# Two buffers in place of one for the query tile in the second part of the differential attention

## The chip, the cores and the metric

The kernel runs on one core of a Trainium2 chip. The metric is the device time of one launch in microseconds (us). Most executions of a kernel agree within 0.3%. Engine names in the views are PE (TensorE, matmuls), PEld (its weight loads), DVE (VectorE), ACT (ScalarE), POOL (GpSimd) and SP (SyncE). All transfers between memory and the on-chip buffer in this kernel are issued by SP, which serves its queue in order.

## The reference

One layer of a hybrid streaming encoder is computed for a prompt of 2048 tokens and a sample of 32 tokens, all in float32. Group A of the attention is a differential attention with four heads: each head has two query and key maps of 64 dimensions and one value of 128.

```python
def diff_core(q, k, v, bias, mask, lam):
    s = jnp.einsum('bqhmd,bkhmd->bhmqk', q, k).astype(jnp.float32) * (HEAD_DIM ** -0.5) + bias[:, None]
    s = jnp.where(mask, s, NEG)
    p = jax.nn.softmax(s, axis=-1)
    w = p[:, :, 0] - lam * p[:, :, 1]
    return jnp.einsum('bhqk,bkhe->bqhe', w.astype(v.dtype), v)

def merge(oa, ob, subln_g, out_norm_b, w_out, lam_init):
    ...
    return jnp.concatenate([oa.reshape(B, T, WIDTH_A), ob], axis=-1) @ w_out

def ffn_ple(h, p, g_mlp, w_up, w_down, w_ple_gate, w_ple_proj):
    c = rmsnorm(h, g_mlp)
    h = h + jnp.square(jax.nn.relu(c @ w_up)) @ w_down
    return h + jax.nn.sigmoid(h @ w_ple_gate) * (p @ w_ple_proj)
```

The mask is causal by chunks of 64 tokens, so a later query sees more keys. Group B is a band attention with eight heads over the last eight chunks. Both groups are projected from the normed input by `w_in`, merged by `w_out`, and followed by the MLP and a gated embedding. The queries, keys and values also leave the kernel as outputs.

## The kernel before

**Numbers.** Every matrix product is made in float32 precision from split operands: a value is stored as a rounded high part and a low part, and a product takes three matmuls (`mm3`, lines L168 to L170). In the attention, high and low parts lie in the two halves of the 128 partitions, or in two planes of a tile.

**Order of the stages.** Tokens are worked on in four blocks of 512 (the last with the sample's 32 behind it). The program projects the queries, keys and values of the first half, does the first part of the differential attention (query pairs 0 to 3) with `self.small = True`, then the rest of the projections and the band attention. After that it sets `self.small = False` and opens the pool `a1` for the second part:

```python
JA1 = [(4, 5), (6, 7, 8)]
            with ExitStack() as x:
                pool = opened(x, "a1", 1, side="right")
                for js in JA1:
                    self.attn_a(js, pool, ps_s, ps_t, ps_o)
```

A pair `j` is two query tiles of 128 tokens; pair 8 stands for the sample. For each group of pairs and each of four heads, `attn_a` loads the bias (`ba`) and the keys (`ka`, one buffer: four transfers for pairs 4 and 5, six for pairs 6 to 8), and then handles the pairs one after another: 20 query tiles in all, eight of them at the start of a head. Each pair loads its queries (`q`, by `load_q`, four transfers), makes score matmuls (tile `s`, L545, three accumulators `ps_s`), row maxima, exponentials in `e` (two buffers for the first map, one for the second), the combination of both maps, transposes (`tpp`, L617), and the products with the values (`v`, two buffers, loaded in chunks; L631 to L633). The result is stored to `oT`.

**What runs beside it.** What follows in the program is the output projection of blocks 0 and 1, their MLP (`ups` and `dps`) and the gate of block 1 (`gps`, `pps`), on two accumulators (`mm`). The program's instructions are put in order by a planner when it is built: it plays the program on a model of the chip, and where an engine would be free it takes an instruction that is ready, the earliest in the program first. So the MLP fills the engines while the second part of the attention waits. In the finished program the order on each engine and on SP's queue is fixed. A buffer that is taken again is guarded by a wait.

**Memory.** The query tile has 2 maps x 2 parts x 256 queries of 4 bytes, so 4 KB in each partition. In the program before, the pool `a1` occupies the upper end of each partition's memory from byte 149,728 to 229,344, and the highest pool from the other side that is in use beside it (`uq`, the MLP's) ends at byte 143,904. Between them 5,824 bytes are free.

The band attention calls `load_q` too, but only while `self.small` is true.

Of the kernel before, what the change touches and what calls it, by code (L numbers as in the profile page):

```python
# [13 lines left out]
F32R = mybir.dt.float32r  # L14
# [5 lines left out]
P = 128  # L20
# [112 lines left out]
class Kern:  # L133
# [343 lines left out]

    def load_q(self, pool, gi, t0, n, maps):
        nc = self.nc
        q = pool.tile([P, len(maps), 2, 256], F32R, tag="q", bufs=2 if self.small else 1, name="q")  # L480
        for d in range(2):
            for i, m in enumerate(maps):
                self.dma(
                    q[64 * d : 64 * d + 64, i, :, :n],
                    self.qS[gi, :, 64 * m : 64 * m + 64, t0 : t0 + n].rearrange("l r c -> r l c"),
                )
        return q
# [796 lines left out]
```

## Time and profile before

| | |
|---|---|
| time, median of 3 runs | 3329.38 us (3328.49 to 3332.86) |
| the profiled execution's own time | 3334.02 us |
| its span, first to last instruction | 3332.1 us |
| mean granted TensorE clock | 0.969 |
| PE busy | 3111.6 us (93%) |
| DVE, ACT, POOL busy | 1674.4, 1705.5, 1467.9 us |
| moved by DMA | 488.93 MB, mean 147 GB/s |
| score matmuls of the second part (L545) | from 1367.3 to 2173.8 us |

A row of a group of instructions reads: line, engine, operation, output and inputs by the program's names, shape and count, then busy time and the mean duration in ns, then the idle time of the engine just before them and what ended it. In a timeline, "[2.16 <-DMA q<-qS]" means that the engine was idle for 2.16 us until the load of `q` had landed. A row of the waits gives the total, the number of times and the longest. A row of the windows gives the stretch and its length, the busy time of PE, PEld, DVE, ACT and POOL with the number of instructions in brackets, and then the clock that TensorE was granted, the busy share of the DMA engines and GB/s. A row of the transfers gives the size of one and the median time from its issue to its landing in us. "issue" is time in which an engine waited for nothing that the profile shows, and SPq is SP's queue.

### The profile page before, as it was taken

The page shows a single profiled execution, that of the slowest core. Times are in us where ns is not written, and L with a number is a line of the kernel's source. Part 1 is how long each engine was busy: PE and PEld are TensorE (multiplying, and loading weights), DVE is VectorE, ACT ScalarE, POOL GpSimd, SP SyncE. Part 2 cuts the span into 40 slices and gives each one's busy share as a digit, 9 for nine tenths or more (in the row PEclk, how much of TensorE's full clock was granted, in tenths as well). Part 3 has the DMA queues.
Part 4 walks back from the last instruction along what each step waited for, and adds up shares of the span by engine and source line. Part 5 has one row for each costly group of instructions (what it writes and reads, how often), then busy time and mean ns, then how long its engine had stood idle before and what let it go on. Part 6 is the DMA issues. An engine that isn't in the chain of part 4 may idle for free.

```text
span 3332.1 us, 50114 instructions
## 1 busy us (share of the span) xinstructions
PE 3111.6 (93%) x17881; PEld 2723.4 (82%) x17881; DVE 1674.4 (50%) x3952; ACT 1705.5 (51%) x3717; POOL 1467.9 (44%) x1083
## 2 busy tenths in 40 slices
PE   6988989999999999989899999988989999999998
PEld 6877778889877888778787878877779999999987
DVE  5117777454555544566656665746542322223235
ACT  4226666566665666666666665654443223222245
POOL 4335654432324433534544443555753333333365
PEclk9998899999999999999999999999999999999999
DMA  7488777786788554544644454346631111111133
GB/s 227 160 253 235 214 212 202 213 241 205 209 238 234 159 139 126 143 137 133 197 134 123 129 136 130 121 135 222 181 114 51 45 45 45 45 47 49 45 91 102
DMA packets 519074, 488.93 MB, mean 147 GB/s; under 512 B 37885, under 2 KB 414017, under 8 KB 518825
## 3 DMA queue, kind: packets, MB, share of 16 engines
q1 hardware_dynamic: 518824, 485.73, 50.2%
q8 instruction: 142, 2.33, 0.3%
q14 instruction: 108, 0.88, 0.1%
HBM read 379.06 MB, written 110.49 MB: 147 GB/s over the span
## 4 chain that ended last, share of the span: by engine, by line
PE 71%; DMA 12%; DVE 7%; ACT 3%; issue 3%; POOL 2%; SPq 2%; DVEq 0%; POOLq 0%; ACTq 0%
PE dps L168 6%; PE dps L169 6%; PE dps L170 6%; PE ups L168 6%; PE ups L169 6%; PE ups L170 6%; PE s L545 3%; DMA q<-qS 3%; PE qps L168 3%; PE qps L169 3%; PE qps L170 3%; PE ob L744 2%; PE sb L704 2%; SPq L144 2%; DMA ka<-kS 2%
## 5 line engine op out<-in xcount | busy, mean ns | idle before, releaser
L153 POOL TENSOR_TENSOR wl<-wr,wh 128x1024 fp32r<-128x1024 f32 x338 | 819.8, 2427 | 1027.5 <-ACT wh L149 985.3
L949 DVE TENSOR_TENSOR h<-h,dps 128x512 f32<-128x512 f32 (+1 forms) x640 | 373.1, 585 | 590.9 <-PE dps L170 578.4
L149 ACT ACTIVATE wh<-wr 128x1024 fp32r<-128x1024 f32 x338 | 357.4, 1058 | 539.9 <-PE dps L169 294.8
L168 PE MATMUL dps<-uh,wh 128*128 128x512 f32 (+1 forms) x1280 | 460.6, 360 | 14.8 <-DVE h L949 11.1
L168 PE MATMUL ups<-cH,wh 128*128 128x512 f32 (+1 forms) x1280 | 452.5, 354 | 9.3 <-ACT relu L914 7.7
L170 PE MATMUL dps<-uh,wl 128*128 128x512 f32 (+1 forms) x1280 | 453.0, 355 | 0.0
L169 PE MATMUL dps<-ul,wh 128*128 128x512 f32 (+1 forms) x1280 | 453.0, 354 | 0.0
L170 PE MATMUL ups<-cH,wl 128*128 128x512 f32 (+1 forms) x1280 | 451.9, 353 | 0.0
L169 PE MATMUL ups<-cL,wh 128*128 128x512 f32 (+1 forms) x1280 | 451.9, 353 | 0.0
L168 PEld LDWEIGHTS dps<-uh,wh 128*128 128x128 f32 x1280 | 243.8, 190 | 49.8 <-DVE h L949 16.9
L168 PEld LDWEIGHTS ups<-cH,wh 128*128 128x128 f32 x1280 | 242.2, 189 | 41.3 <-ACT relu L914 7.9
L170 PEld LDWEIGHTS dps<-uh,wl 128*128 128x128 f32 x1280 | 242.9, 190 | 33.4
L169 PEld LDWEIGHTS ups<-cL,wh 128*128 128x128 f32 x1280 | 242.7, 190 | 31.1
L153 POOL TENSOR_TENSOR ul<-relu,uh 128x272 fp32r<-128x272 f32 (+1 forms) x160 | 176.0, 1100 | 206.3 <-ACT uh L149 203.6
L170 PEld LDWEIGHTS ups<-cH,wl 128*128 128x128 f32 x1280 | 242.3, 189 | 30.1
L169 PEld LDWEIGHTS dps<-ul,wh 128*128 128x128 f32 x1280 | 243.2, 190 | 27.0
L545 PE MATMUL s<-ka,q 128*128 128x256 f32 (+4 forms) x784 | 197.2, 357 | 50.4 <-DMA q<-qS 29.1
L168 PE MATMUL qps<-aH,wh 128*128 128x512 f32 (+1 forms) x640 | 230.2, 360 | 6.6 <-ACT wh L149 2.2
L169 PE MATMUL qps<-aL,wh 128*128 128x512 f32 (+1 forms) x640 | 228.3, 357 | 0.0
L170 PE MATMUL qps<-aH,wl 128*128 128x512 f32 (+1 forms) x640 | 227.9, 356 | 0.0
L559 ACT ACTIVATE e<-s,nm 128x512 f32<-128x512 f32 (+3 forms) x256 | 155.2, 611 | 102.7 <-DVE nm L551 65.2
L545 PEld LDWEIGHTS s<-ka,q 128*128 128x128 f32 (+1 forms) x784 | 137.4, 200 | 78.5 <-issue 27.3
(217 smaller groups left out, 7076.9 us busy)
## 6 DMA issues: line engine op xcount, KB each, us to landing
wr<-w_up SPq DMA_DIRECT2D x96, 512.0 KB, 4.2
wr<-w_down SPq DMA_DIRECT2D x96, 512.0 KB, 3.7
wr<-w_in SPq DMA_DIRECT2D x74, 512.0 KB, 4.9
q<-qS SPq DMA_DIRECT2D x256, 128.0 KB, 4.7
v<-vSa SPq DMA_DIRECT2D x64, 512.0 KB, 3.8
ka<-kS SPq DMA_DIRECT2D x32, 512.0 KB, 7.2
wr<-w_out SPq DMA_DIRECT2D x32, 512.0 KB, 5.0
wr<-w_ple_gate SPq DMA_DIRECT2D x32, 512.0 KB, 4.4
```

The lines of the kernel that those rows point to most:

```text
L144: self.nc.sync.dma_start(dst, src)
L149: nc.scalar.activation(hi, raw, AF.Copy)
L153: eng.tensor_tensor(lo, raw, hi.bitcast(F32), op=ALU.subtract)
L168: nc.tensor.matmul(ps, lh, rh, start=start and i == 0, stop=False)
L169: nc.tensor.matmul(ps, lh, rl, start=False, stop=False)
L170: nc.tensor.matmul(ps, ll, rh, start=False, stop=stop and i == n - 1)
L545: nc.tensor.matmul(s, q[:, m, hl, P * qi : P * qi + nr], kt[:, m, k0 : k0 + n], start=hl == 0, stop=hl == 1)
L559: nc.scalar.activation(dst, src, AF.Exp, bias=nmx, accum_out=z[:nr, m, bi : bi + 1])
L704: nc.tensor.matmul(s, q[:, 0, hl, P * qi : P * qi + nr], kt[:, c : c + w], start=hl == 0, stop=hl == 1)
L744: nc.tensor.matmul(o[:, qa:qb], vt, pt[:kn, i - kfirst, qa:qb], start=x == 0 and y == 0, stop=x == len(order) - 1 and y == 1,)
L949: nc.vector.tensor_tensor(hv, hv, ps, op=ALU.add)
```

## The change

`load_q` asks for two buffers of the query tile whatever `self.small` is. Only the second part of the differential attention had one; in the first part and in the band attention there were two before. The pool `a1` grows by 4,096 bytes in each partition.

```diff
     def load_q(self, pool, gi, t0, n, maps):
         nc = self.nc
-        q = pool.tile([P, len(maps), 2, 256], F32R, tag="q", bufs=2 if self.small else 1, name="q")
+        q = pool.tile([P, len(maps), 2, 256], F32R, tag="q", bufs=2, name="q")
         for d in range(2):
             for i, m in enumerate(maps):
```

## The prediction, made before the changed kernel was built

> **What bounds the kernel now.** I read the page first, for the engine that carries the span; then the waits of that engine in the stretch that the change touches; then single instructions at the places found.
>
> ```profile
> span 3332.1 us, 50114 instructions
> PE 3111.6 (93%) x17881; PEld 2723.4 (82%) x17881; DVE 1674.4 (50%) x3952; ACT 1705.5 (51%) x3717; POOL 1467.9 (44%) x1083
> PEclk9998899999999999999999999999999999999999
> L545 PE MATMUL s<-ka,q 128*128 128x256 f32 (+4 forms) x784 | 197.2, 357 | 50.4 <-DMA q<-qS 29.1
> ```
>
> TensorE is busy for 93% of the span and no other engine for much over half. So the time is TensorE's work, plus its idle time, plus what it loses at a reduced clock. The score matmuls (L545) have 50.4 us of idle time ahead of them, most of it ended by a query load. The changed tile is used from 1357 us to 2174 us, so the next view is that stretch with its margins: first the busy times, then TensorE's waits in it, then who waited for the query tile.
>
> ```profile
> 1350.00:2240.00 890.00, 829.31 (x4120) 691.16 (x4119) 552.58 (x1146) 540.67 (x1232) 419.59 (x304) 0.97 0.49 138
> PE s L545 <- DMA q<-qS: 27.3, 11, 4.1
> PE dps L168 <- DVE h L949: 11.1, 11, 2.0
> PE s L545 <- issue: 4.1, 1, 4.1
> PE s L545 <- ACT e L559: 2.9, 2, 2.6
>   PE s L545: 31.4, 12
> ```
>
> TensorE is idle for 890.0 − 829.3 = 60.7 us of this stretch. The query tile is behind 31.4 us of it, in 12 places: the 27.3 us and the one of 4.1 us that the waits put down to "issue". The rest of the stretch is attention mixed with the MLP of the first half, which fills TensorE while attention waits.
>
> **Two kinds of stall.** The loop makes a difference between them. A pair inside a head needs only a new query tile. The first pair of a head needs new keys (`ka`, one buffer) as well. These are the pairs of the first kind that stall, and three of the second kind (least, a long one, most):
>
> ```profile
> 1482.84 0.41 PE L545 MATMUL s<-ka,q 128*128 128x384 f32 x1 [2.16 <-DMA q<-qS]
> 1665.57 0.59 PE L545 MATMUL s<-ka,q 128*128 128x384 f32 x2 [1.21 <-DMA q<-qS]
> 1761.85 0.77 PE L545 MATMUL s<-ka,q 128*128 128x512 f32 x1 [2.96 <-DMA q<-qS]
> 1999.80 0.47 PE L545 MATMUL s<-ka,q 128*128 128x512 f32 x1 [3.62 <-DMA q<-qS]
> 1367.27 1.74 PE L545 MATMUL s<-ka,q 128*128 128x512 f32 x6 [0.18 <-DMA q<-qS]
> 1833.62 0.80 PE L545 MATMUL s<-ka,q 128*128 128x512 f32 x1 [3.74 <-DMA q<-qS]
> 2072.16 2.04 PE L545 MATMUL s<-ka,q 128*128 128x512 f32 x4 [4.14 <-issue]
> ```
>
> The four inside heads sum to 9.95 us. The eight at head starts hold the other 31.4 − 9.95 = 21.45 us, 2.7 us each. A stall of about 3 us has a second price. Seven times in this stretch the clock is at half beside such a stall. The rows are the first of the seven, the two that belong to stalls inside heads, the sum of all seven, and a stretch behind the 2.16 us stall, where the clock stayed full:
>
> ```profile
> 1450.76:1454.17 3.41, 3.41 (x9) 2.79 (x9) 3.07 (x6) 0.78 (x2) 0.00 (x0) 0.50 0.46 169
> 1761.37:1764.78 3.41, 2.93 (x7) 2.38 (x8) 1.83 (x4) 3.08 (x6) 0.22 (x1) 0.50 0.45 154
> 2000.30:2003.71 3.41, 3.41 (x9) 2.67 (x8) 2.56 (x4) 1.79 (x4) 1.51 (x1) 0.50 0.36 138
> sum 27.29, PE 23.98 PEld 19.70 DVE 10.86 ACT 6.68 POOL 1.74; mean PE 3.43 PEld 2.81 DVE 1.55 ACT 0.95 POOL 0.25
> 1483.00:1486.00 3.00, 3.00 (x15) 2.60 (x15) 2.54 (x5) 0.79 (x2) 2.92 (x4) 1.00 0.48 175
> ```
>
> Half of the busy time at half clock is lost: 23.98 / 2 = 12.0 us, of which (2.93 + 3.41) / 2 = 3.2 us belong to stalls inside heads and 8.8 us to head starts. So the query tile costs 31.4 + 12.0 = 43.4 us now: 13.1 us inside heads, 30.3 us at head starts. That is the ceiling of what is removed directly.
>
> [...]
>
> **The change, part by part.** No instruction is added or removed. What moves are the four DMA issues of each query tile:
>
> ```profile
> L144 SPq DMA_DIRECT2D q<-qS x80: 573/605/1467, 1357.4 to 2169.5; - x80
> ```
>
> That is 20 tiles in 812 us, 41 us for a pair.
>
> *Inside heads.* With one buffer the load is issued when the last score matmul of the pair before has read the tile:
>
> ```profile
> 1476.34 0.25 PE s L545 x2
> 1476.60 0.59 SPq L144
> 1477.89 4.81 DMA q<-qS
> 1482.84 0.41 PE s L545
> ```
>
> From the release (1476.6) to the next score matmul 6.2 us pass: three issues and a landing of 4.8 us. With two buffers the next tile's slot is free a whole pair earlier; a pair takes 41 us on average, so 6.2 us are covered several times over. All 9.95 us and the 3.2 us of clock go: −13.1 us. What is late next is a slot of scores or exponentials; that wait is in the list above with 2.9 us in two places. It already paces the pairs behind their first score blocks, and MLP matmuls stand behind it in the order.
>
> *Head starts.* Here the keys are released by the same last score matmul and are loaded ahead of the queries:
>
> ```profile
> 1817.76 4.58 SPq L144 DMA_DIRECT2D ka<-kS  x6
> 1822.38 4.16 SPq L144 DMA_DIRECT2D q<-qS  x4
> ka<-kS SPq DMA_DIRECT2D x24, 512.0 KB, 6.9
> q<-qS SPq DMA_DIRECT2D x64, 128.0 KB, 5.7
> 1517.25 6.47 DMA ka<-kS
> 1523.73 6.99 DMA q<-qS
> ```
>
> Now the queries come 15.9 us after the release (1817.76 to 1833.62), and TensorE, filled by MLP work, arrives at the score matmul 3.74 us before that, 12.1 us after the release. With the change the queries are there long before, and the score matmul waits for the keys alone. The first score block needs the fourth of six key issues. Six take 4.58 us, so the fourth is out about 2.3 to 3.1 us after the release, and at the median landing of 6.9 us its data are there 9.5 to 12 us after it. If TensorE still arrived at 12.1 us, nothing would be left of the head-start stalls: −30.3 us, one end. But the order of TensorE's queue is fixed when the program is built, by a planner that places a matmul where it expects its data. Inside heads it had TensorE there after 4.1 us (1476.6 to 1482.84 − 2.16) where 6.2 passed; at the head start after 12.1 where 15.9 passed: 0.66 to 0.76 of the real time. Without the queries it will place the score matmul earlier. By the same ratios the stall on the keys comes to 9.5 × (1 − 0.76) = 2.3 us up to 12 × (1 − 0.66) = 4.1 us, 3.2 us in the middle, against 2.7 us today: +4 us for the eight, and +11 us at the other end. If the miss goes with the number of transfers, six in place of ten, it falls to 1.6 us: −9 us. I take −3 us, about the middle of −9 and +4, and leave the clock's 8.8 us where they are.
>
> *DMA issues moved.* Each group of four occupies SP's queue for 2.5 to 4.2 us, now in the middle of a pair instead of its end. What is queued behind it are value loads and weight loads. TensorE's waits in the stretch name no such load, so their lead hides this: 0, and up to 2.5 us at a place or two if that lead is gone. At a head start the queue becomes shorter by the same amount.
>
> *The order behind attention.* Attention's chain gets shorter, by up to 6 us at each of 19 tiles, so it ends earlier, and more of block 1's gate runs after it and alone, on two accumulators. The end of the stage shows what that is like:
>
> ```profile
> 2175.00:2240.00 65.00, 56.72 (x269) 45.98 (x269) 25.24 (x44) 33.44 (x63) 39.71 (x32) 0.95 0.39 117
> 2241.61 0.50 PE L168 MATMUL gps<-hH,wh 128*128 128x512 f32 x1 [3.75 <-DVE sm L994]
> ```
>
> In these 65 us TensorE idles for 8.3 us, 13% against 7% over the whole stage. If some 60 us more of the stage ran at 13%, that would cost 60 × 0.06 = 4 us; if the work that is left covers attention's last steps instead, it gains about as much. I take +2 us, with −4 to +8 as bounds (the upper one if all eight steps of the gate stall by 1 us more).
>
> **Sum.** −13.1 − 3 + 0 + 2 = −14 us. On the profiled execution's own 3334.0 us (span 3332.1 and 1.9 around it) that gives 3320 us. That execution lies 4.6 us above the median of the runs; on the median of 3329.4 the forecast is 3315 us. The likeliest case by itself spans 3300 to 3322: −13 inside heads, −12 to +4 at head starts, −4 to +2 behind attention.
>
> **The rivals.**
>
> *Everything goes.* The order stays about as it is, TensorE reaches each head's first score matmul when the keys have landed, and no stall is left: −43.4 us, 3286 us. For it speaks that 12.1 us of filler lie at the head start shown, and the keys need 9.5 to 12; against it, that the planner moves the score matmul as soon as it believes the keys to be there.
>
> *The stalls change their name.* Inside heads 13 us go; the keys' stall grows by 4 us in all; and the gate, run alone, costs the full 8 us: −1 us, 3328 us, not to be told from no change. For it speaks the row of 3.75 us before a gate matmul; against it, that this row is one of few.
>
> *Slower: the keys take over, and worse.* The score matmul at a head start now hangs on the largest transfer of the stage alone, with no small load behind it to hold it back in the planned order. If the planner counts on the keys much too early, TensorE stands still before them. Break-even: eight stalls, each with one half-clock stretch of 3.41 us (1.7 us lost), must cost 43.4 us in all, so 5.4 us each, a stall of 3.7 us. At 6 us each it is 8 × 7.7 = 61.6 us, +18 us, 3347 us. For it speaks that the misses already measured (0.66 to 0.76 of the real time) give 3.2 us, not far under break-even, and 4.1 us at their end; against it, that the same misses at head starts come out at 2.7 us on average today with ten transfers, and would be on six.
>
> *The change does nothing.* SP serves its queue in order, and it waits for other things most of the time. A query load that is free to go but stands behind a weight load's wait comes late again:
>
> ```profile
> SPq L144 <- POOL wl L153: 293.0, 72, 10.0
> ```
>
> The longest such wait is 10.0 us, though, and the load has a pair's 41 us; only a planner that leaves the load at its old place in the order would make this true. It gives 3329 us, and I count it with the case before it.
>
> **How the numbers follow.** Forecast 0.45, everything goes 0.15, stalls change their name or nothing happens 0.17, slower 0.23. About 0.2% (7 us) is what a measurement of this kernel can tell from no change. So: faster 0.45 + 0.15 = 0.60, the same 0.17, slower 0.23. I give slower this much because the order of every queue in the stage is planned anew, and the break-even stall is only 0.5 us above the computed one. The range has its low end at the case where everything goes, 3285 us. Its high end is 3340 us, +11 us: it holds the milder half of the slower case, a stall of about 5.1 us at each head start (8 × 6.8 = 54.4 against 43.4).
>
> **What the profile after would show.** Right: the score matmuls (L545) have under 25 us of idle time ahead of them in the whole run against 50.4; the four stalls inside heads are gone, and no stall there is put down to `q`; query issues in SP's timeline stand amid the value loads of the pair before, and no longer behind the keys; what is left at head starts is put down to `ka`, 2 to 4 us each; attention's last score matmul comes before 2174 us. Wrong: query loads still right behind the last score matmul (the load was not moved); stalls on `ka` above 3.7 us on average (the slower rival); score matmuls that wait for exponentials (`e`) in more than a few places; or gate matmuls with several us of idle time each after attention's end.

## The result and the profile after

The kernel with two query buffers takes 3311.8 us (median of 4 runs, 3304.5 to 3314.0) against 3329.1 us (3328.5 to 3332.9) before: a ratio of 0.994, with a 95% interval of 0.9925 to 0.9955. That is 17 us faster by the medians and 15 to 25 us by the interval; the forecast was 3315 us. The profiled execution took 3310.7 us, its mean granted clock is 0.975 against 0.969. First the same lines of the page as before, with the row of the down-projection added:

```profile
span 3308.8 us, 50118 instructions
PE 3096.1 (94%) x17881; PEld 2710.5 (82%) x17881; DVE 1669.4 (50%) x3952; ACT 1698.4 (51%) x3717; POOL 1468.8 (44%) x1083
PEclk9999899999999999999999999999999999999999
L545 PE MATMUL s<-ka,q 128*128 128x256 f32 (+4 forms) x784 | 192.7, 348 | 40.8 <-issue 15.7
L168 PE MATMUL dps<-uh,wh 128*128 128x512 f32 (+1 forms) x1280 | 459.7, 359 | 22.0 <-DVE h L949 16.7
```

The idle time ahead of score matmuls fell from 50.4 to 40.8 us, by far less than the 31.4 us that the query tile was behind. TensorE's busy time fell by 15.5 us with the same 17881 matmuls: that is the clock, since half of its busy time at half clock goes from 79.5 to 62.0 us over the whole profile. Now the windows' row of the stretch:

```profile
1350.00:2240.00 890.00, 833.39 (x4182) 695.49 (x4182) 560.00 (x1155) 545.99 (x1247) 428.96 (x310) 0.99 0.51 143
```

Then TensorE's waits in it, and last the sum of those that the query tile ended:

```profile
PE dps L168 <- DVE h L949: 16.7, 14, 3.1
PE s L545 <- issue: 8.5, 2, 5.7
PE s L545 <- DMA ka<-kS: 6.5, 3, 3.8
PE s L545 <- ACT e L559: 5.7, 4, 3.9
PE s L545 <- DMA q<-qS: 1.7, 1, 1.7
  PE s L545: 1.7, 1
```

By this list the query tile is behind 1.7 us in place of 31.4. The two places put down to "issue" have to be read by the landings: there, as at the other stalls on a load, the score matmul starts some 0.1 us after the transfer that it needs has landed. The stall of 2.8 us ends so with the third key transfer, and the one of 5.7 us with the third query transfer, shown below. So the query tile is still behind 7.4 us in two places, and the keys are behind 9.4 us (6.5 and 2.8). The exponentials have more waits (5.7 against 2.9 us), and the MLP's down-projection `dps` waits longer for VectorE's accumulation into `h` (16.7 against 11.1 us). The groups of the same stage, before and then after, say the same (the last columns are idle time and what ended it):

```profile
L168 PE MATMUL dps<-uh,wh 128*128 128x512 f32 x382 | 158.6, 415 | 13.3 <-DVE h L949 11.1 <-DVE nm L557 1.3 <-ACT relu L914 0.9
L545 PE MATMUL s<-ka,q 128*128 128x512 f32 (+3 forms) x528 | 137.1, 364 | 35.1 <-DMA q<-qS 27.3 <-issue 4.1 <-ACT e L559 2.9
```

```profile
L168 PE MATMUL dps<-uh,wh 128*128 128x512 f32 x382 | 157.7, 413 | 20.3 <-DVE h L949 16.7 <-ACT relu L914 3.2 <-ACT sqacc L884 0.3
L545 PE MATMUL s<-ka,q 128*128 128x512 f32 (+3 forms) x528 | 134.5, 355 | 23.3 <-issue 8.5 <-DMA ka<-kS 6.5 <-ACT e L559 5.7
```

For an account I cut both profiles at the same work: from the second part's first score matmul to the end of block 1's gate, 4069 matmuls in both. The stage's row comes first, then the sum over all its half-clock stretches; before, then after:

```profile
1367.27:2249.00 881.73, 819.60 (x4069) 683.29 (x4070) 556.42 (x1148) 538.54 (x1230) 415.83 (x301) 0.97 0.49 139
sum 51.17, PE 46.95 PEld 37.83 DVE 28.09 ACT 23.36 POOL 12.66; mean PE 3.61 PEld 2.91 DVE 2.16 ACT 1.80 POOL 0.97
```

```profile
1364.19:2228.80 864.61, 808.13 (x4069) 675.13 (x4070) 555.63 (x1148) 533.91 (x1230) 414.06 (x301) 0.99 0.50 141
sum 23.88, PE 21.72 PEld 18.48 DVE 12.53 ACT 7.29 POOL 7.47; mean PE 3.62 PEld 3.08 DVE 2.09 ACT 1.21 POOL 1.25
```

TensorE's idle time goes from 881.73 − 819.60 = 62.1 to 56.5 us. The clock's loss, half of the busy time at half clock, goes from 23.5 to 10.9 us (15 stretches of 3.41 us, then 7). So the stage is 17.1 us shorter in these two profiles, and 12.6 us of that are the clock. The rest of the profiled 23.3 us lies outside the stage, half before and half after it. About 6 of the 23.3 us are only the choice of executions: before's profiled one lies 4.9 us above its median, the one after 1.1 us below.

| us, in the stage | before | after | change | forecast |
|---|---|---|---|---|
| score stalls inside heads | 9.95 | 0 | −9.95 | −9.95 |
| score stalls at head starts | 21.5 | 15.8 | −5.7 | −3 |
| clock beside those stalls | 12.0 | 4.3 | −7.7 | −3.2 |
| TensorE's other idle time | 30.7 | 40.7 | +10.0 | +2 |
| clock elsewhere | 11.5 | 6.6 | −4.9 | 0 |
| TensorE's work at full clock | 796.1 | 797.3 | +1.1 | 0 |

The timeline shows what the first row of this table is, a pair inside a head that no longer stalls, and the three longest stalls that are left at head starts:

```profile
1745.90 0.39 PE L545 MATMUL s<-ka,q 128*128 128x512 f32 x1
1442.41 1.10 PE L545 MATMUL s<-ka,q 128*128 128x512 f32 x3 [3.84 <-DMA ka<-kS]
1523.11 0.70 PE L545 MATMUL s<-ka,q 128*128 128x512 f32 x2 [2.83 <-issue]
1932.72 0.77 PE L545 MATMUL s<-ka,q 128*128 128x512 f32 x1 [5.68 <-issue]
```

SP's queue at two head starts shows how the load moved:

```profile
1795.19 2.54 SPq L144 DMA_DIRECT2D q<-qS  x4
1798.41 3.84 SPq L144 DMA_DIRECT2D ka<-kS  x6
1802.29 6.02 SPq L144 DMA_DIRECT2D q<-qS  x4
```

```profile
1916.40 1.24 SPq L144 DMA_DIRECT2D q<-qS  x2
1917.68 3.85 SPq L144 DMA_DIRECT2D ka<-kS  x6
1921.58 8.33 SPq L144 DMA_DIRECT2D q<-qS  x6
q<-qS SPq DMA_DIRECT2D x1, 128.0 KB, 11.1
```

At the first of them, the four issues ahead of the keys are the queries of the head's first pair. The four behind the keys are those of the second pair, which nobody needs yet. At the second head start only two of the first pair's four transfers got ahead of the keys. The last row is the next of them, the one issued at 1921.58: it landed 11.1 us later, at 1932.6, and with it the stall of 5.68 us ends (1932.72 above). The needed key transfer had been complete since 1929.3 by the trace's semaphore events, so the keys alone would have left a stall of about 2.4 us.

The reason is which slot comes free. With two buffers a pair takes the slot of the pair before the last one. In heads of two pairs that slot has been free for about a pair's length: the queries of the score matmul at 1442.41 were issued from 1389.84 on. In heads of three pairs, the last pair is the sample's. Its four score matmuls took only from 1916.44 to 1917.63, so the slot of the pair before it came free 1.3 us ahead of the keys, and 3.2 and 1.9 us ahead at the two other such places.

### The profile page after: what moved, and what is told of

Its sections match the earlier page's. It is cut to its first block, busy times and chain, and to the rows that moved or that the text cites. A ratio compares the mean times of both kernels' runs of the same rounds, so it can differ in the third digit from the quotient of the medians.

```text
span 3308.8 us, 50118 instructions
## 1 busy us (share of the span) xinstructions
PE 3096.1 (94%) x17881; PEld 2710.5 (82%) x17881; DVE 1669.4 (50%) x3952; ACT 1698.4 (51%) x3717; POOL 1468.8 (44%) x1083
## 5 line engine op out<-in xcount | busy, mean ns | idle before, releaser
L168 PE MATMUL dps<-uh,wh 128*128 128x512 f32 (+1 forms) x1280 | 459.7, 359 | 22.0 <-DVE h L949 16.7
L545 PE MATMUL s<-ka,q 128*128 128x256 f32 (+4 forms) x784 | 192.7, 348 | 40.8 <-issue 15.7
L545 PEld LDWEIGHTS s<-ka,q 128*128 128x128 f32 (+1 forms) x784 | 135.7, 195 | 66.4 <-issue 27.9
```

Source lines behind the costliest of these rows:

```text
L168: nc.tensor.matmul(ps, lh, rh, start=start and i == 0, stop=False)
L545: nc.tensor.matmul(s, q[:, m, hl, P * qi : P * qi + nr], kt[:, m, k0 : k0 + n], start=hl == 0, stop=hl == 1)
```

## Experiments

**Is it the memory layout?** The pool `a1` also grew by 4 KB. A padding tile of that size goes into it, and the query tile keeps its one buffer.

```diff
-                pool = opened(x, "a1", 1, side="right")
+                pool = opened(x, "a1", 1, side="right"); nc.gpsimd.memset(pool.tile([P, 1024], F32, tag="pad", name="pad")[:, 0:1], 0.0)
```

> One query buffer as before, and beside it an unused tile of 4 KB in the pool of the second part, so that the pool has the size and place that it has with two buffers. The order of TensorE's and SP's queues is that of the kernel before. Theory (the gain comes from loading the query tile a pair early): nothing of that is here, 3329 us like before, with the query tile still behind about 31 us of TensorE's idle time in 12 places. Rival (the gain comes from where the pool's tiles lie, or from what they have to wait for): close to the changed kernel, 3312 us.

3330.4 us, ratio 1.000 (0.9989 to 1.0012). The row of those who wait for the query tile is nearly that of before:

```profile
  PE s L545: 29.9, 11
```

So these runs show no effect of the layout, to within 4 us either way. The order on TensorE and on SP is that of the kernel before, and yet the profile has 18 half-clock stretches in the stage against 15. By so much the count of one profile can differ without any change of order.

**The two halves of the change.** The pool holds two tiles with a name each, and a counter chooses between them (set up by two one-element instructions on POOL, not shown). In the first kernel the tile changes only at pairs inside a head, so the first pair of a head waits for the pair before it as it did; in the second kernel it changes only at the first pair of a head.

```diff
-        q = pool.tile([P, len(maps), 2, 256], F32R, tag="q", bufs=2 if self.small else 1, name="q")
+        q = pool.tile([P, len(maps), 2, 256], F32R, tag="q" if self.small else f"q{self.slot}", bufs=2 if self.small else 1, name="q")
...
+                self.slot = 0 if self.small else self.slot ^ (j != js[0])   # second kernel: j == js[0]
                 self.attn_a_pair(g, j if j < 8 else None, kt, ba, pool, ps_s, ps_t, ps_o)
```

> Two query slots, used so that only pairs inside a head change the slot; the first pair of a head takes the slot of the pair before it, so its load waits for that pair's last score matmul, as before the change. Theory: the stalls inside heads go (10.0 us of idle time and 3.2 us of clock in the trace of before), the ones at head starts stay as before (21 us in 8 places, with their half-clock stretches): -13 us, 3316 us. Rival (the gain is the planner's new order at large and belongs to no place): the time of the changed kernel or anything else, and no tie between the places where the slot changes and the stalls that go.

> The other half: the slot changes only at the start of a head, so the first pair's queries are loaded early and come before the keys; inside a head the load waits for the pair before, as before the change. Theory: the stalls inside heads stay (about 10 us of idle time), those at head starts are ended by the keys and fall from 21 us to about 16 us as in the trace of the changed kernel, with some of the clock: -3 to -8 us, 3321 to 3326 us; this half and the other add up to about the whole change (-17 us). Rival (the planner's new order at large): no such sum, either half anywhere between 3305 and 3335 us.

Inside heads alone: 3321.6 us, ratio 0.9982 (0.9972 to 0.9991), −6 us. The four stalls are gone, but the head starts went from 21.5 to 24.4 us, 19.9 of them still on queries behind keys (who waits for the query tile, and the longest of these in the timeline):

```profile
  PE s L545: 19.9, 6
```

```profile
1520.00 2.72 PE L545 MATMUL s<-ka,q 128*128 128x512 f32 x6 [5.47 <-DMA q<-qS]
```

Head starts alone: 3314.5 us, ratio 0.9959 (0.9946 to 0.9972), −14 us. Head starts went to 15.4 us, and the half-clock stretches from 15 to 7. The slot changes once a head here, so it is free early, and at all seven later heads the four query transfers are issued ahead of the keys. Where the changed kernel kept its stall of 5.68 us on the queries, 2.49 us are left, and the keys end them:

```profile
1917.68 2.54 SPq L144 DMA_DIRECT2D q<-qS  x4
1922.50 3.83 SPq L144 DMA_DIRECT2D ka<-kS  x6
1933.95 0.93 PE L545 MATMUL s<-ka,q 128*128 128x512 f32 x3 [2.49 <-DMA ka<-kS]
```

The surprise is inside the heads, where this kernel loads as late as before and yet idles for 2.2 us in place of 9.95. One such pair, on TensorE and SP:

```profile
1744.94 0.41 PE L545 MATMUL s<-ka,q 128*128 128x256 f32 x2
1745.52 2.54 SPq L144 DMA_DIRECT2D q<-qS  x4
1751.34 0.86 PE L545 MATMUL s<-ka,q 128*128 128x512 f32 x3
```

The load is issued behind the last score matmul, and the next score matmul starts 5.8 us later. In the kernel before, the same load was issued at 1755.83 and the score matmul started 6.0 us later, with a stall of 2.96 us (the prediction's row at 1761.85). The load is no faster; the planner put 5.8 us of other work there in this order, and 3.1 us in that one. So a late load alone did not make these stalls: the place the planner gave the score matmul did too.

The halves add up to −20 us, about the whole. But the sizes are the reverse of the forecast: it put 13 us inside heads and 3 at head starts. Nor is the second half a clean one: its order also lost most of the stalls inside heads, and it loads the first pair's queries earlier than the whole change does. So that the two add up does not show what each place is worth.

**Keys by chunks.** Most of what is left at head starts waits for keys, and the first score block needs the fourth of six key transfers (the third of four in heads of two pairs). Now the two loops around them change places, so that it needs the second.

```diff
-            for hl in range(2):
-                src = self.kS[g, hl].rearrange("(m r) c -> r m c", m=2)
-                for c0 in range(0, nk, 1024):
-                    c1 = min(c0 + 1024, nk)
+            for c0 in range(0, nk, 1024):
+                c1 = min(c0 + 1024, nk)
+                for hl in range(2):
+                    src = self.kS[g, hl].rearrange("(m r) c -> r m c", m=2)
```

> The changed kernel with the keys' transfers in another order: both halves of the first 1024 keys first, so that the first score block's keys come with the second transfer of a head and not with the third of four or the fourth of six. Theory (what is left at head starts, 15.8 us in the trace of the changed kernel, is the landing of the keys, and a planner that counts on it too early): the time from the keys' release to the first score matmul falls from about 11 to 12 us to about 8 us; the planner moves the matmul forward too, so that part of the stall stays: 2 to 10 us faster than the changed kernel, about 3306 us. Rival (the planner's miss does not shrink with the wait): the same stalls at other times, 3312 us.

With two query buffers: 3298.6 us, ratio to before 0.9909 (0.9896 to 0.9921), faster than both kernels, and 13 us below the changed one where 2 to 10 were expected. Part of the reason is the expected one: in five of the seven later heads the score matmul runs 8.5 to 10.1 us after the first key issue, where the changed kernel took 10.9 to 12.3 us in six of them. The first two rows show the shortest of these, without a stall. In the other two heads the stall is on queries again (4.69 us in the last row, and 4.81 us put down to "issue"), because two of the first pair's four transfers stand behind the six of the keys:

```profile
1910.27 3.87 SPq L144 DMA_DIRECT2D ka<-kS  x6
1918.76 0.71 PE L545 MATMUL s<-ka,q 128*128 128x512 f32 x2
1808.23 1.22 PE L545 MATMUL s<-ka,q 128*128 128x512 f32 x2 [4.69 <-DMA q<-qS]
```

The head-start stalls still sum to 15.6 us against 15.8: what the keys end fell from 9.4 to 6.1 us, and what the queries end rose from 5.7 to 9.5. Of the 10.4 us of idle time that this stage lost against the changed kernel, 8.5 us lie ahead of `dps` (20.3 to 11.8 us). So most of that idle time fell away at another place than the one that was aimed at.

> One query buffer as before, with the keys' transfers in the other order (both halves of the first 1024 keys first). The order of the four computing engines is the same as in the kernel before, only SP's differs. With one buffer the queries still come behind all key transfers, so the first score matmul of a head cannot start earlier: 3330 us within 3 us by the theory that what counts at a head's start is the last transfer that the score matmul waits for. Rival (the order of the key transfers gains by itself): 3315 us or less.

With one query buffer the same edit gives 3327.4 us, 0.9987 (0.9975 to 0.9998), −4 us, and the query tile is behind nearly as much waiting as before:

```profile
  PE s L545: 27.2, 10
```

**Other orders of the planner.** By now each edit had moved time in places that it did not touch. To see how much of the 17 us is the buffer and how much the order that came with it, an instruction that multiplies by one is put into the program, once with one query buffer and once with two. It makes the planner arrange everything anew. Three places were used: the attention's reciprocals, 64 columns of the combined exponentials, and the MLP of blocks 0 and 1. In the traces it stands 32, 36 and 64 times there and takes 0.17, 0.18 to 0.19 and 0.7 us in the median; the expectation of the second had put it at 40 times.

```diff
                 nc.vector.reciprocal(rz[:nr], rz[:nr])
+                self.small or nc.vector.tensor_scalar(rz[:nr], rz[:nr], 1.0, None, op0=ALU.mult)
```

> One query buffer as before. [...] Theory (the second buffer gains because the load is early): 3330 us within 5 us, query stalls of some 25 to 35 us and 13 to 17 half-clock stretches remain. Rival (any new order of the stage moves the time by as much as the change did): 10 us or more away from 3330.

> Two query buffers, with the first added instruction (the product by 1 behind the sum). A new order of the stage with early loads. Theory: 3312 us within 6 us, no stall inside heads, and some 15 us at head starts that the keys end. Rival (luck of the order): anywhere between 3300 and 3335 us, not clear of the one-buffer kernels.

```diff
+            self.small or nc.vector.tensor_scalar(e[0][:nr, 0:64], e[0][:nr, 0:64], 1.0, None, op0=ALU.mult)
             ws.append(e[0])
```

> One query buffer as before, and another instruction that changes no value, in another place: a product by 1 of 64 columns of each combined probability tile, 40 in the stage. A second new order of the stage. Theory: 3330 us within 5 us, as for the other one. Rival (any new order moves the time by as much as the change): 10 us or more away from 3330, and another way than the first.

> Two query buffers, with the second added instruction (the product by 1 of 64 columns). Theory: 3312 us within 6 us, below both one-buffer kernels with added instructions by 12 us or more. Rival (luck of the order): overlaps them.

```diff
                     nc.scalar.activation(r, r, AF.Square)
+                    len(blocks) > 1 or nc.vector.tensor_scalar(r[:, 0:64], r[:, 0:64], 1.0, None, op0=ALU.mult)
```

> One query buffer as before; the added instruction without effect on values (a product by 1 of 64 columns, VectorE) now stands in the MLP of blocks 0 and 1, the work that fills TensorE beside attention, and not in attention's chain. A third new order of the stage. Theory of the early load: 3330 us within 5 us. Theory that the order's luck is as large as the change (from the runs with instructions added to attention: 3332 and 3318 us with one buffer, 3331 and 3331 with two): anywhere from 3312 to 3335 us.

> Two query buffers with the instruction added to the MLP, not to attention's chain. Theory of the early load: 3312 us within 6 us, and the two kernels with two buffers that came out at 3331 us lost their gain to the instructions added to attention's own chain. Theory of the order's luck: anywhere from 3305 to 3335 us; no stall inside heads in either case.

> Two query buffers and the other order of the key transfers (3299 us without more), with the instruction added to the MLP: a second order of the stage for this version. If its 30 us come from the shorter wait at head starts: 3300 us within 8 us. If they were mostly the luck of one order: back between 3310 and 3330 us.

"Behind q" is the idle time of score matmuls that the query tile ended in 1350 to 2240 us, with the stalls put down to "issue" that end with a landing of queries. Idle and half-clock stretches are those of the stage in the one profiled execution, which can lie up to 13 us from the median (3345 us with the reciprocals and one buffer). Ratios are to the kernel before.

| order | buffers | time, us | ratio (95%) | behind q | idle | half-clock |
|---|---|---|---|---|---|---|
| as written | 1 | 3329.1 | 1 | 31.4 | 62.1 | 15 |
| | 2 | 3311.8 | 0.9940 (0.9925 to 0.9955) | 7.4 | 56.5 | 7 |
| MLP instruction | 1 | 3325.9 | 0.9985 (0.9974 to 0.9997) | 25.3 | 56.9 | 13 |
| | 2 | 3305.9 | 0.9927 (0.9912 to 0.9941) | 6.1 | 49.9 | 7 |
| reciprocals | 1 | 3332.2 | 0.9994 (0.9981 to 1.0007) | 19.6 | 66.5 | 13 |
| | 2 | 3331.2 | 1.0000 (0.9984 to 1.0015) | 4.0 | 61.9 | 13 |
| 64 columns | 1 | 3318.4 | 0.9952 (0.9937 to 0.9968) | 19.2 | 48.6 | 10 |
| | 2 | 3331.4 | 1.0001 (0.9987 to 1.0015) | 3.2 | 57.1 | 11 |
| keys by chunks | 1 | 3327.4 | 0.9987 (0.9975 to 0.9998) | 28.0 | 57.0 | 16 |
| | 2 | 3298.6 | 0.9909 (0.9896 to 0.9921) | 10.7 | 46.1 | 7 |
| chunks, MLP instruction | 2 | 3302.3 | 0.9911 (0.9896 to 0.9927) | 7.5 | 50.1 | 8 |

The second buffer takes most of the query tile's wait away in every order; what is left stands at head starts behind the sample's pair. What the time does is another matter: −17, −20, −1 and +13 us by the medians, and −29 us where the keys come by chunks. The expected 3312 us within 6 us came out in none of the three added orders with two buffers: 3306, just outside, and 3331 twice, as the rival (luck of the order) allows. With the instruction on 64 columns two buffers are slower than one, and the intervals do not touch. These are the waits of that two-buffer kernel, and then its hand-over from block 1's gate to the next stage:

```profile
PE dps L168 <- DVE h L949: 21.7, 16, 3.9
PE s L545 <- DMA ka<-kS: 11.3, 4, 4.8
```

```profile
2229.00:2420.00 191.00, 164.65 (x859) 139.04 (x858) 113.01 (x134) 84.75 (x147) 118.18 (x63) 0.95 0.66 205
```

All of `dps`'s idle time in its stage is 24.1 us, against 7.3 us with one buffer and the same instruction. Its hand-over is 191 us long, against 177 us in the changed kernel, but the one-buffer kernel of that order has 192 us, so the hand-over is not what the second buffer costs. Over the five pairs the second buffer changed the idle time ahead of `dps` by +7, +4, −7, +17 and −1 us: it has no fixed sign, and follows the order. Why the two instructions inside the attention's own chain (reciprocals, columns) lost the gain while the one in the MLP did not stays open: a longer chain and the luck of the order would both look like this.

The two edits together hold up under the second order that was tried, at 0.9911 against 0.9909. What the keys by chunks add there is not clear of noise: with the MLP instruction and two buffers it is 3302.3 us with them and 3305.9 without, and the intervals overlap.

## Why the prediction was right, and where only in sum

**The bound and the removed wait: right, but for two places.** TensorE's idle time and its clock set the time of the stage; the four stalls inside heads are gone in the changed kernel, and in all six two-buffer kernels they sum to 0.06 us at most. The loads inside heads are a pair early, as the argument had it. At head starts the prediction said that the queries would be there long before. Behind the sample's pair that failed: the slot came free only 1.3 to 3.2 us ahead of the keys, and 7.4 us of waiting for queries are left.

**Inside heads, −13.1: right in the trace, too large as an effect.** Done alone it gave −6 us (−3 to −9). Its working took each stall as a property of the late load. The kernel with only the head starts changed shows that an order exists in which the same late load is covered by 5.8 us of other work, and in the one with only the inside changed the head starts grew from 21.5 to 24.4 us.

**Head starts, −3, clock left at 8.8: the step that was mis-sized.** The stall is 2.0 us on average, near the 2.3 us that −3 us stands for, but there is luck in it. The prediction's own terms, 2.3 to 3.1 us and a landing of 6.9 us, add up to 9.2 to 10.0 us, not to its 9.5 to 12. Where the keys end the wait or none is left, the needed key transfer landed 10.7 to 12.2 us after the first key issue, and the score matmul came at 10.9 to 12.3 us. And the mean hides stalls from 0 to 5.7 us, the longest of which is not one on the keys. Done alone the head starts were worth −14 us. The larger failure is the clock: it was left at its value of today, and beside both kinds of stall it fell from 12.0 to 4.3 us. This is the sum of the windows beside the head-start stalls of the changed kernel that ran at half clock, three cells of 3.41 us from 1443.02 and 1931.12 us on (half of 8.64 is lost):

```profile
sum 10.24, PE 8.64 PEld 7.70 DVE 3.02 ACT 0.64 POOL 0.00; mean PE 4.32 PEld 3.85 DVE 1.51 ACT 0.32 POOL 0.00
```

**DMA issues moved, 0: right for what it looked at.** In the changed kernel no score matmul waits for a value or weight load. What it did not look at are the queries themselves, which stand behind the keys in part at two head starts: there one stall is 5.7 us where the keys alone would have left about 2.4, and another 1.7 us.

**Behind attention, +2 with −4 to +8: the wrong place and too small.** Attention's last score matmul came 24 us earlier (2149.9 against 2174.1 us) and the gate ended 20 us earlier, with 5.6 us of its own stalls against 5.5. The bound looked at the gate; what was late next was `dps` on VectorE's `h` (+7 us), and score matmuls behind the first of a pair (+4 us, 1.7 of them on queries).

**The sum** of −14 us is near the measured −17 because its errors cancel: +10 us where +2 stood, against −13 us of clock where −3 stood. The orders with one instruction more show that the sign was not safe either: of the three, one kept the gain, one lost it and one turned it round. The chance of 0.23 for slower was not too much caution, though its mechanism, keys above 3.7 us on average, was not seen at head starts in any of these kernels; the slower order stalls on `dps`, which no rival named.

**The markers.** Query stalls gone, and `ka` in their place: right inside heads and for 9.4 us at head starts, but 7.4 us on queries are left. "Under 25 us ahead of L545 in the whole run": wrong by its own making, since 15.3 of the 50.4 us lay outside the stage; inside it went from 35.1 to 23.3. "Query issues no longer behind the keys": issues still stand there, mostly those of the next pair, but three of the first pair's own at two head starts. "Put down to `ka`, 2 to 4 us each": the four on keys are 1.0 to 3.8 us. Scores waiting for `e`: four places in place of two, 5.7 us.

## What to carry to other kernels

A second buffer moves a load back to the release of the pair before the last, so look how long the pair in between is: behind the short one here it was only 1.3 to 3.2 us. It took away most of its wait in every order here, but where a planner sets the order anew the time that comes out differs by as much as the edit is worth: here one buffer gave 3318 to 3332 us and two gave 3306 to 3331 us over four orders, so try an edit under a few orders (an instruction that multiplies by one makes another) before believing half a per cent. Look for what the first consumer really waits for, and let its pieces come first. Count the half-clock stretches beside the idle time; in the two profiles here they were the larger part of the gain.

## What the runs showed of the hardware

**The clock changes on a fixed grid of 3.41 us, and the length of a gap alone does not tell how.** In each of the 14 profiles the starts of the half-clock stretches lie on a grid of 3.413 us, within 0.006 us. The grid begins anywhere from 0.09 to 3.24 us behind the span's start. What the clock of the next cell goes with is how much of one cell of this grid TensorE idles. Five cells of the changed kernel, in two groups:

```profile
1688.78:1692.19 3.41, 1.35 (x6) 1.04 (x6) 3.41 (x5) 1.83 (x6) 1.26 (x1) 1.00 0.22 45
1692.19:1695.60 3.41, 3.41 (x12) 2.95 (x12) 2.50 (x9) 2.00 (x8) 2.40 (x4) 0.50 0.28 109
1518.11:1521.52 3.41, 1.66 (x6) 1.05 (x6) 3.21 (x6) 2.04 (x4) 0.14 (x1) 1.00 0.99 184
1521.52:1524.94 3.42, 1.83 (x11) 1.65 (x12) 1.75 (x4) 0.00 (x0) 0.00 (x0) 1.00 1.13 247
1524.94:1528.35 3.41, 3.41 (x20) 2.85 (x18) 2.55 (x5) 1.51 (x3) 0.00 (x0) 1.00 0.74 254
```

A gap of 2.06 us lay wholly in the first cell, which idles for 3.41 − 1.35 = 2.06 us, and the next cell runs at half clock. The gap of 2.83 us at a head start fell across a border, 1.75 and 1.59 us of idle time with other small gaps, and the clock stayed full. Over the stretch from 1340 to 2300 us of all 14 profiles, of the full-clock cells with 1.91 us or more of idle time 127 of 127 are followed by half clock; of those with some idle time but less than 1.6 us, 3 of 642; of the 45 between, 14. So a length of about 3 us, at which the prediction put a stall's second price, is not the line: the gap of 2.06 us cost 1.7 us more, half of the 3.41 us that TensorE was busy in the cell behind it, and the one of 2.83 us nothing more, by where they fell.

**The place on the grid differs from one profile to the next**, and this may be much of the spread of a kernel's times: over 184 timed executions, each taken against its own kernel's mean, time and mean granted clock go together with a correlation of −0.66, 2 us for 0.001 of clock. That is a correlation and not more. It also says that the clock's part in the result is not one profile's accident: 75 executions of the kernel before have a mean clock of 0.970, the four of the changed one 0.974.
